# Three more token tiles of a gated block's input turned on VectorE and through DRAM, with the work around them put in another order

## The chip, the core and the metric

The kernel runs on one core of one Trainium2 chip. A core has five engines, each with a queue of its own that is worked off strictly in order: TensorE (PE, matmuls into PSUM; the profile shows its weight loads apart, as PEld), VectorE (DVE), ScalarE (ACT), GpSimd (POOL) and SyncE (SP, which here only issues DMA transfers). Engines wait for one another through semaphores. The metric is the time of one execution on the device in microseconds (us); lower is better. Every number below that has no other source is from the profile or the trace of the kernel before.

## The reference

One layer of a hybrid block over 1040 tokens (16 learned meta tokens ahead of 1024 real ones), width 1024, all in float32:

```python
mix = mixer(rms_norm(h, pre_mix_norm), w_in, ..., w_out)     # short convolutions, a gate, layer norm
h = h + rms_norm(mix, post_mix_norm)
ff = swiglu(rms_norm(h, pre_ffn_norm), w_gate, w_up, w_down) # silu(xn @ w_gate) * (xn @ w_up) @ w_down
h = h + rms_norm(ff, post_ffn_norm)
return h[:, N_META:, :]
```

`w_gate` and `w_up` are 1024 x 2816, `w_down` is 2816 x 1024. The change lies at the seam between the mixer's output projection (`w_out`) and the gate's two matrix products.

## The kernel before

**Arithmetic.** Every float32 operand is kept as two parts, a rounded `hi` and a rest `lo = x - hi`; a product is three matmuls (hi*hi, lo*hi, hi*lo; `mm3`, lines 107 to 109). The rounding is a cast on ScalarE, the rest a subtraction on VectorE, so each operand of TensorE costs one instruction on either engine. The products of the gate and of `w_down` are done by a scheme of the Strassen-Winograd kind: the operands are cut into 2 x 2 blocks, and seven products of sums of blocks replace eight.

**Up to the seam.** The 1024 tokens are eight tiles of 128. `group` (line 852) multiplies the mixer's output `y` (`yh`, `yl`) by `w_out` for a few token tiles at a time: tiles 0 to 2, then 3 to 5, then 6 and 7. The contraction runs over eight blocks k of 128; for each k there are 12 matmuls for two tiles. A dictionary gives a function to run ahead of step 0, 1, 2, ... of that loop; step 6 stands for the last two blocks, which are done tile by tile. `group` ends with `leave_psum`: ScalarE takes the sum of squares of each PSUM bank (line 621), VectorE multiplies it by a gain (line 622), and the bank is free. Tile 7's two sums lie in banks 7 and 4 (`OUT_BANKS`).

`norms` then makes two RMS norms of each tile and adds the residual: line 643 on VectorE, the squares of line 645 on ScalarE, and line 651 on VectorE, which gives the gate's input `hn` of the tile with tokens on the partitions.

**Turning.** The gate's products need `hn` with channels on the partitions. Tiles 0, 1 and 2 are turned by `send`, `fetch` and `receive`: VectorE transposes 32 x 32 blocks (line 669), SP writes the tile to DRAM (`xd`, line 670), four DMAs read it back with the blocks in their places into the same `hn` tile (line 675), and ScalarE copies it into `raw` (line 685) and, for the upper channel half of tiles 0 to 3, also makes `B11`'s hi and lo (lines 683, 684). Tiles 3 to 7 are turned by TensorE in `turn`: eight transposes each (line 659) into a PSUM bank, copied out by ScalarE (lines 661, 663). Tile 3's transposes stand ahead of step 5 of `group((6, 7))`, those of tiles 4 and 5 ahead of its step 6 (`early`), those of 6 and 7 behind the third product of the gate.

**The gate's products.** `raw[q, g]` are the blocks of the turned input (q: channel half, g: token half), called `r11`, `r21`, `r12`, `r22`. `Pair(j)` holds 128 columns of `w_gate` (m = 0) and of `w_up` (m = 1) from either half; 11 pairs. `order` is the order written out by hand of the 77 steps s = (pair, product): the seven products of pairs 0 and 1 alternate, then each pair has its seven in a row. A step is 24 matmuls, 12 for m = 0 and 12 for m = 1. Its weights side is made `LEAD = 2` steps ahead by `a_side(s)`: sums of blocks on VectorE, the cast on ScalarE (line 710), the rest on VectorE (line 697). Its right side is one of seven pairs of tiles `X[n]`: `X[1] = B11`, `X[2] = B21` (a hi and lo of `r21`), `X[6] = T2`, and so on. The results leave PSUM a step later (`results`, `Pair.leave`); the gate itself is `glu`: a Silu on ScalarE and a product, on GpSimd. In the text below, "step 0" is pair 0's product 1, step 1 pair 1's product 1, steps 2 and 3 product 2 of each (on `B21`), steps 4 and 5 product 6 (on `T2`, made of all eight tiles).

Step 1 writes banks 7 and 4, those that tile 7 of `group((6, 7))` leaves. Steps 2 and 3 add onto the banks of steps 0 and 1, so that ScalarE must first have copied these out (line 794).

**What sets the order.** Every engine's queue is written out by hand: instructions stand in each queue in the order in which the program makes them (`manual_schedule`). Buffers come from pools with a fixed number of places; an instruction that first writes a new tile waits until a place of that pool has been left by all users of the old tile, also by those that the program makes later on other queues. Four pools matter here:

- `tp`, tag "t", 5 places of one token tile each: `gB_post` and `gB_ffn` (the two gains, used by lines 622 and 651 to the end of `norms((6, 7))`), the `hn` tiles, and some of the weights of the pairs: by the condition in `Pair.load` the `w_up` block of pair 1's first half (`u11` below) is one.
- `wp`, tag "ws", 3 places: raw rows of `w_out`, and the other weights of pairs 0 and 1. Pair 0's two blocks and pair 1's `w_gate` block take the places that rows 5, 6 and 7 of `w_out` leave when they are split (`split_o`, lines 161 and 162).
- `yap`, the places of `y`; `xg` and `rp`, places of 8 KB a partition for `raw`, the `X` tiles and others.

## Time and profile before

| | |
|---|---|
| median of 3 runs | 963.99 us (963.87 to 964.51) |
| the profiled execution, its own time | 964.56 us |
| its span in the profile | 962.8 us |
| granted TensorE clock | 0.999 |
| DVE, ACT, POOL busy | 76%, 42%, 27% of the span |

The profile's page, its views by window and line, the waits and the chain of waits are all of that one execution. Times in the views are us from the start of the span. A row of the timeline is: start, length, engine and line, operation, out<-in by the program's names, shapes, how many instructions are merged (the length is then that of all of them), and in brackets the idle time of the engine before it and what ended that. The page gives a matmul of 512 columns 0.39 us; consecutive ones start 0.227 us apart, since they are pipelined.

### The profile page before, as it was taken

The page shows a single profiled execution, that of the slowest core. Times are in us where ns is not written, and L with a number is a line of the kernel's source. Part 1 is how long each engine was busy: PE and PEld are TensorE (multiplying, and loading weights), DVE is VectorE, ACT ScalarE, POOL GpSimd, SP SyncE. Part 2 cuts the span into 40 slices and gives each one's busy share as a digit, 9 for nine tenths or more (in the row PEclk, how much of TensorE's full clock was granted, in tenths as well). Part 3 has the DMA queues.
Part 4 walks back from the last instruction along what each step waited for, and adds up shares of the span by engine and source line. Part 5 has one row for each costly group of instructions (what it writes and reads, how often), then busy time and mean ns, then how long its engine had stood idle before and what let it go on. Part 6 is the DMA issues. An engine that isn't in the chain of part 4 may idle for free.

```text
span 962.8 us, 12522 instructions
## 1 busy us (share of the span) xinstructions
PE 954.6 (99%) x4570; PEld 820.2 (85%) x4570; DVE 735.4 (76%) x1022; ACT 405.2 (42%) x666; POOL 260.1 (27%) x225
## 2 busy tenths in 40 slices
PE   9999999999999999999999999999999999999997
PEld 9999999998888888888888888888888888888885
DVE  6699999886476799999987787887886543546775
ACT  8533423365446653453443343333433333322341
POOL 1277954552000000204134133132242111111210
PEclk9999999999999999999999999999999999999999
DMA  8011111114447510555532633624419899856866
GB/s 312 23 45 46 65 45 44 66 44 151 134 155 250 185 67 1 186 228 173 222 151 106 225 125 117 238 91 152 154 39 366 295 356 365 260 175 212 319 205 247
DMA packets 60878, 159.83 MB, mean 166 GB/s; under 512 B 6417, under 2 KB 8977, under 8 KB 60817
## 3 DMA queue, kind: packets, MB, share of 16 engines
q1 hardware_dynamic: 44352, 106.98, 30.8%
q0 software_dynamic: 11088, 40.38, 13.1%
q10 hardware_dynamic: 5376, 11.67, 3.4%
q8 instruction: 36, 0.59, 0.3%
q14 instruction: 26, 0.20, 0.1%
HBM read 108.67 MB, written 50.33 MB: 165 GB/s over the span
## 4 chain that ended last, share of the span: by engine, by line
PE 98%; DMA 1%; DVE 0%; SPq 0%; ACT 0%; issue 0%; DVEq 0%
PE x L108 8%; PE x L109 8%; PE x L107 8%; PE y L108 6%; PE y L109 6%; PE y L107 6%; PE qx L108 4%; PE qx L107 4%; PE qx L109 4%; PE qy L108 3%; PE qy L107 3%; PE qy L109 3%; PE po L107 3%; PE po L109 3%; PE po L108 3%; PE p_c L107 2%
## 5 line engine op out<-in xcount | busy, mean ns | idle before, releaser
L697 DVE TENSOR_TENSOR op<-u,op 128x512 fp32r<-128x512 f32 x154 | 141.6, 951 | 27.8 <-ACT op L710 26.7
L710 ACT CAST op<-u 128x512 fp32r<-128x512 f32 x154 | 92.0, 619 | 133.2 <-DVE u L697 75.2
L697 DVE TENSOR_TENSOR db<-wb,db 128x512 fp32r<-128x512 f32 x77 | 54.0, 704 | 86.2 <-ACT db L1174 85.9
L700 POOL TENSOR_TENSOR C<-C,C 128x512 f32<-128x512 f32 x11 | 17.3, 1569 | 322.9 <-ACT C L822 210.7
L1174 ACT CAST db<-wb 128x512 fp32r<-128x512 f32 x77 | 47.3, 621 | 119.7 <-PE qx L109 57.2
L107 PE MATMUL qx<-db,a 128*128 128x512 f32 x176 | 68.5, 389 | 0.0
L108 PE MATMUL qx<-db,a 128*128 128x512 f32 x176 | 68.5, 389 | 0.0
L109 PE MATMUL qx<-db,a 128*128 128x512 f32 x176 | 68.5, 389 | 0.0
L694 DVE TENSOR_TENSOR U<-y,U 128x512 f32<-128x512 f32 x66 | 43.5, 682 | 17.0 <-PE y L109 17.0
L700 POOL TENSOR_TENSOR U<-U,U 128x512 f32<-128x512 f32 x21 | 30.1, 1434 | 86.9 <-ACT U L822 60.5
L108 PE MATMUL qy<-db,a 128*128 128x512 f32 x132 | 51.5, 390 | 0.0
L109 PE MATMUL qy<-db,a 128*128 128x512 f32 x132 | 51.4, 389 | 0.0
L107 PE MATMUL qy<-db,a 128*128 128x512 f32 x132 | 51.3, 389 | 0.0
L1054 POOL DMA_DIRECT2D a<-gdS x44 | 23.2, 528 | 91.4 <-PE qx L109 45.6
L382 DVE SCALAR_TENSOR_TENSOR ac<-g,pr,ac 128x512 f32<-128x512 f32 x56 | 42.0, 750 | 0.0
L382 DVE SCALAR_TENSOR_TENSOR ae<-d,pr,ae 128x512 f32<-128x512 f32 x56 | 42.0, 750 | 0.0
L107 PEld LDWEIGHTS qx<-db,a 128*128 128x128 f32 x176 | 33.0, 188 | 6.9
L109 PEld LDWEIGHTS qx<-db,a 128*128 128x128 f32 x176 | 33.0, 188 | 6.9
L108 PEld LDWEIGHTS qx<-db,a 128*128 128x128 f32 x176 | 33.0, 188 | 6.8
L697 DVE TENSOR_TENSOR u<-u,u 128x512 f32<-128x512 f32 x44 | 38.0, 884 | 0.8
L1054 POOL DMA_DIRECT2D a<-gdA x33 | 17.8, 539 | 61.7 <-PE qx L109 26.8
L107 PE MATMUL x<-B21h,op 128*128 128x512 f32 x88 | 34.3, 390 | 0.0
(358 smaller groups left out, 2928.0 us busy)
## 6 DMA issues: line engine op xcount, KB each, us to landing
a<-gdS POOLq DMA_DIRECT2D x44, 512.0 KB, 4.5
a<-gdA POOLq DMA_DIRECT2D x33, 512.0 KB, 5.8
u<-w_gate_u SPq DMA_DIRECT2D x22, 512.0 KB, 5.4
u<-w_up_u SPq DMA_DIRECT2D x22, 512.0 KB, 6.2
gdS<-HI SPq DMA_DIRECT2D x44, 256.0 KB, 2.4
gdA<-HI SPq DMA_DIRECT2D x33, 256.0 KB, 2.0
gdS<-GS SPq DMA_DIRECT2D x33, 256.0 KB, 2.7
ws_o<-w_out_u SPq DMA_DIRECT2D x14, 512.0 KB, 4.6
```

The costliest lines, as they stand in the source:

```text
L107: nc.tensor.matmul(o, lh, rh, start=start, stop=False, skip_group_check=again)
L108: nc.tensor.matmul(o, lh, rl, start=False, stop=False, skip_group_check=again)
L109: nc.tensor.matmul(o, ll, rh, start=False, stop=stop, skip_group_check=again)
L382: nc.vector.scalar_tensor_tensor(out if i == n - 1 else acc, src[:, i : i + HALF], w(i), init if i == first else acc, op0=ALU.mult, op1=AL ...
L694: (eng or nc.vector).tensor_tensor(o, a, b, op=ALU.add)
L697: (eng or nc.vector).tensor_tensor(o, a, b, op=ALU.subtract)
L700: (eng or nc.vector).tensor_tensor(o, a, b, op=ALU.mult)
L710: nc.scalar.copy(t[:, 0, :], src)
L1054: nc.gpsimd.dma_start(loads[n, j], gd[an][j])
L1174: nc.scalar.copy(t[:, 0, :], b)
```

## The change

- **Turning.** Tiles 3, 4 and 5 go the way of tiles 0 to 2. `norms` hands its last products (line 651) back as a list for this group, so that tile 3's product and transpose come first and tiles 4 and 5 follow inside `group((6, 7))`: step 1 has the split of row 5 of `w_out` and tile 5's product, step 2 the split of row 6, the loads of pair 0, the four reads of tile 3 and tile 4's transpose and write, step 3 the split of row 7, a load of pair 1 and tile 5's transpose and write. The reads of tiles 4 and 5 are issued in `early`, behind the load of `u11`; `receive(3)` is in `early`, `receive(4)` and `receive(5)` where the cast of `B21` was. The transposed tiles `xt` take places that `y` leaves.
- **B21** is cast and its rest made at the end of `early`, ahead of `leave_psum` in the queues, in place of inside `norms((6, 7))`. The sums `t1_sum` of the first two column blocks move from `early` to behind `a_side(3)`.
- **Pairs 0 and 1** multiply their gate on VectorE in place of GpSimd.
- **Operand sums ahead of results:** from step 3 on, `a_side(s + 2)` is cut in two; its sums and casts (`a_high`) stand ahead of the results of step s - 1, its rests (`a_low`) stay behind them.
- **Places:** `y` lies in a pool `rp` of four places that stays open (tag of `big`), `rq` has one, and `T2`, `B22` and a block of `w_down` are given to other pools.

```diff
         side_of(a).tensor_tensor(cv[a], cv[a], rS, op=ALU.mult)
 
     def after_b(a):
-        yh[a], yl[a] = (yap.tile([P, SEQ], F32R, tag="y", name=f"y{c}{a}") for c in "hl")
+        y = big(f"y{a}", pool=rp)
+        yh[a], yl[a] = y[:, :SEQ], y[:, SEQ:]
         for q in range(2):
             s = slice(q * HALF, (q + 1) * HALF)
             nc.vector.tensor_tensor(cv[a][:, s], pu["b", a][:, q, :], cv[a][:, s], op=ALU.mult)
...
         if i == 0:
             fs.close()
             ya = ExitStack()
-            yap = ya.enter_context(tc.tile_pool(name="yap", bufs=8, side="right"))
+            rp = ctx.enter_context(tc.tile_pool(name="rp", bufs=4, side="right", reuse_waits="tile"))
     assert next(conv_taps, 0) == 0
     split_o(1, nc.gpsimd)
     load_o(2)
...
         nc.sync.dma_start(h, x[i * P : (i + 1) * P, :])
         return h
 
-    def norms(grp, left, s1, hs, between=None, first=None):
-
+    def norms(grp, left, s1, hs, between=None, first=None, parts=False):
         n_ = len(grp)
         v = sm.tile([P, 16], F32, tag="s2", name=f"pm{grp[0]}")
         nc.vector.tensor_tensor(v[:, :n_], s1[:, 0:n_], s1[:, 4 : 4 + n_], op=ALU.add)
...
         if between:
             between()
         r = rsqrt_n(v2[:, :n_], 1.0 / D, RMS_EPS, n_, f"pf{grp[0]}")
-        for q, i in enumerate(grp):
-            nc.vector.scalar_tensor_tensor(n[i], hs[i], r[:, q : q + 1], gB["ffn"], op0=ALU.mult, op1=ALU.mult)
+        last = [lambda q=q, i=i: nc.vector.scalar_tensor_tensor(n[i], hs[i], r[:, q : q + 1], gB["ffn"], op0=ALU.mult, op1=ALU.mult) for q, i in enumerate(grp)]
+        if parts:
+            return n, last
+        for f in last:
+            f()
         return n
 
     def turn(i, n, at=(0, 1)):
...
                 nc.tensor.transpose(pt[:, k * P : (k + 1) * P], n[:, (4 * q + k) * P : (4 * q + k + 1) * P], ident)
             p4 = pt.rearrange("p (a b) -> p a b", a=4)
             nc.scalar.copy(raw[q, i // 4][:, :, c], p4)
-            if (q, i // 4) == (0, 0):
-                nc.scalar.copy(B11[0][:, :, c], p4)
-                nc.vector.tensor_tensor(B11[1][:, :, c], p4, B11[0][:, :, c].bitcast(F32), op=ALU.subtract)
-
-    xd = {i: dram.tile([P, D], F32, tag=f"xd{i}", name=f"xd{i}") for i in range(3)}
+
+    xd = {i: dram.tile([P, D], F32, tag=f"xd{i}", name=f"xd{i}") for i in range(6)}
 
     def send(i, n, t):
         nc.vector.transpose(t.rearrange("p (j k q) -> p j k q", j=4, k=8), n.rearrange("p (k j q) -> p j k q", k=8, j=4))
...
             nc.sync.dma_start(n[32 * j : 32 * j + 32].rearrange("r (i x) -> r i x", i=4), src)
 
     def receive(i, n):
-        c = slice(i * P, (i + 1) * P)
+        c = slice((i % 4) * P, (i % 4 + 1) * P)
         split4 = lambda t: t[:, :, c].rearrange("p k (i q) -> p k i q", i=4)
         for q in range(2):
             n4 = n.rearrange("p (i k q) -> p k i q", i=4, k=8)[:, 4 * q : 4 * q + 4]
-            if q == 0:
+            if q == 0 and i < 4:
                 nc.scalar.copy(split4(B11[0]), n4)
                 nc.vector.tensor_tensor(split4(B11[1]), n4, split4(B11[0]).bitcast(F32), op=ALU.subtract)
-            nc.scalar.copy(split4(raw[q, 0]), n4)
+            nc.scalar.copy(split4(raw[q, i // 4]), n4)
 
     st = None
     free = [5, 6, 7, 4, 0, 1, 2, 3]
...
             if m == 0:
                 nc.scalar.activation(v[c, 0], v[c, 0], AF.Silu)
             else:
-                mul(v[c, 0], v[c, 0], v[c, 1], None if (self.j, c) == (NP - 1, "U2") else nc.gpsimd)
+                mul(v[c, 0], v[c, 0], v[c, 1], None if self.j < 2 or (self.j, c) == (NP - 1, "U2") else nc.gpsimd)
 
         def split(self, *names):
 
...
 
     hs = {i: residual_x(i) for i in (3, 4, 5)}
     s1, left = group((3, 4, 5), middle, {1: ahead(0, 5), 2: ahead(1, 6), 3: lambda: [ahead(2, 7)(), back(0)()], 4: back(1), 5: back(2)})
-    hn = norms((3, 4, 5), left, s1, hs)
+    hn, last_mul = norms((3, 4, 5), left, s1, hs, parts=True)
+
+    def turned(i):
+        t = big(f"xt{i}", F32, rp)[:, :D]
+        send(i, hn[i], t)
+
+    last_mul[0]()
+    turned(3)
+    last_mul[1]()
 
     n_hi = [0]
     X = {1: B11}
...
 
     order = [(j, n) for n in (1, 2, 6, 5, 7, 3, 4) for j in range(2)]
     order += [(j, n) for j in range(2, NP) for n in (1, 6, 2, 5, 7, 3, 4)]
-    made, sums = {}, {}
+    made, high, sums = {}, {}, {}
     LEAD = 2
 
-    def a_side(s, *places):
+    def a_high(s, *places):
         if s >= len(order) or s in made:
             return
         j, n = order[s]
         if j > 1 and n == 1 and j + 1 < NP:
             pairs[j + 1] = Pair(j + 1)
         src = sums.pop(s, None) or [pairs[j].a_side(n, m) for m in range(2)]
-        t = [operand_hi(src[m], f"{n}_{j}{m}", places[m] if places else None) for m in range(2)]
-        for m in range(2):
-            sub(t[m][:, 1, :], src[m], t[m][:, 0, :].bitcast(F32))
-        made[s] = t
-
-    def pairs_load():
+        made[s] = [operand_hi(src[m], f"{n}_{j}{m}", places[m] if places else None) for m in range(2)]
+        high[s] = src
+
+    def a_low(s):
+        for m, src in enumerate(high.pop(s, ())):
+            sub(made[s][m][:, 1, :], src, made[s][m][:, 0, :].bitcast(F32))
+
+    def a_side(s, *places):
+        a_high(s, *places)
+        a_low(s)
+
+    def step1():
+        ahead(5)()
+        last_mul[2]()
+
+    def step2():
+        split_o(6)
+        pairs[0].load(0)
+        fetch(3, hn[3])
+        turned(4)
+
+    def step3():
         split_o(7)
         pairs[1].load(0, (0,))
+        turned(5)
 
     def early():
         for q in range(2):
             raw[q, 1] = blocks(big(f"raw{q}1", F32))
-        turns(4, 5, at=(5, 6))()
         pairs[1].load(0, (1,))
-        for i in range(2):
-            t1_sum(i)
+        for i in (4, 5):
+            fetch(i, hn[i])
+        back(3)()
         a_side(0)
         a_side(1, (hp, "h"), (jp, "jk"))
+        X[2] = pair("B21", (rp, rp))
+        copy_hi(X[2], raw[1, 0])
+        split_lo(X[2], raw[1, 0])
 
     hs = {i: residual_x(i) for i in (6, 7)}
-    s1, left = group((6, 7), up, {1: ahead(5), 2: lambda: [split_o(6), pairs[0].load(0)], 3: pairs_load, 5: turns(3), 6: early})
+    s1, left = group((6, 7), up, {1: step1, 2: step2, 3: step3, 6: early})
     r11, r21, r12, r22 = raw[0, 0], raw[1, 0], raw[0, 1], raw[1, 1]
-    X[2] = pair("B21", (None, None))
     T2r = blocks(big("T2r", F32))
     results = {s: pairs[order[s][0]].product(order[s][1], made.pop(s)) for s in range(2)}
 
     def between():
         pairs[0].load(1)
         results[0]()
-        split_lo(X[2], r21)
         a_side(2)
 
-    hn = norms((6, 7), left, s1, hs, between, lambda: copy_hi(X[2], r21))
+    turned_back = hn
+    hn = norms((6, 7), left, s1, hs, between, lambda: [receive(i, turned_back.pop(i)) for i in (4, 5)])
     del left, hs
     table(AF.Silu)
     ya.close()
     p2.close()
-    rp = ctx.enter_context(tc.tile_pool(name="rp", bufs=5, side="right", reuse_waits="tile"))
+    rq = ctx.enter_context(tc.tile_pool(name="rq", bufs=1, side="right", reuse_waits="tile"))
     st = ctx.enter_context(tc.tile_pool(name="st", bufs=11, reuse_waits="tile"))
-    X[6] = pair("T2", (rp, rp))
+    X[6] = pair("T2", (rq, None))
     a_side(3)
-    for f in (t2_sum, t2_hi, t2_lo):
+    for f in (t1_sum, t2_sum, t2_hi, t2_lo):
         for i in range(2):
             f(i)
 
...
 
     def b22():
         T4.append(blocks(big("T4h")))
-        X[3] = pair("B22", (rp, None))
+        X[3] = pair("B22", (None, None))
         copy_hi(X[3], r22)
         split_lo(X[3], r22)
 
...
     def load_b(b, g):
 
         n_ = min(4, NP - 4 * g)
-        pool = {(0, 0): bp, (0, 1): bp, (0, 2): rp, (1, 0): rp, (2, 1): rp, (2, 2): rp, (3, 1): rp}.get((b, g))
+        pool = {(0, 0): bp, (0, 1): bp, (0, 2): rq, (1, 0): rp, (2, 1): rp, (2, 2): rp, (3, 1): rp}.get((b, g))
         t = WB[b, g] = blocks(big(f"wb{b}{g}", F32, pool))
         src = w_down[4 * g : 4 * g + n_, :, b // 2, b % 2 * 512 : (b % 2 + 1) * 512]
         for k in range(n_) if b == 0 else (slice(0, n_),):
...
         if s == len(order) - 1:
             load(1, "A11", 2, "ws")
             load(1, "A11", 3, "wh")
+        if s > 2:
+            a_high(s + LEAD)
         results.pop(s - 1, lambda: None)()
         if s == 2:
             for f in (t1_sum, t2_sum):
...
                 load(1, "A11", q, "ws")
         for f in extra.get(s, ()):
             f()
-        a_side(s + LEAD)
+        a_low(s + LEAD)
         if s in (13, 16):
             pairs[s == 16].sums()
         if s in first_splits:
```

## The prediction, made before the changed kernel was run

> **What bounds the kernel now.** First the page: its share of busy time, then the chain of work that ended last.
>
> ```profile
> span 962.8 us, 12522 instructions
> PE 954.6 (99%) x4570; PEld 820.2 (85%) x4570; DVE 735.4 (76%) x1022; ACT 405.2 (42%) x666; POOL 260.1 (27%) x225
> ...
> PE 98%; DMA 1%; DVE 0%; SPq 0%; ACT 0%; issue 0%; DVEq 0%
> ```
>
> Next PE's waits, all of them:
>
> ```profile
> PE warm L89 <- DVE pr L113: 1.1, 1, 1.1
> PE p_g L108 <- DVE xl L179: 0.3, 1, 0.3
> ```
>
> Both are on its first matmuls (`warm`, and `p_g`, the first unit). After that TensorE waits for nobody, so the kernel is as long as TensorE's list of work: an instruction taken off PE shortens it by its step, as long as nothing makes PE wait, and any new wait of PE is added in full. A view by windows then says how near such waits are.
>
> ```profile
> 340.00:360.00 20.00, 20.00 (x98) 16.77 (x97) 19.50 (x31) 12.69 (x22) 0.00 (x0) 1.00 0.22 79
> ```
>
> Its columns are the window's sum, then busy us (instructions) of PE, PEld, DVE, ACT and POOL, the granted clock and the DMA's share: VectorE is busy for 19.5 of 20 us. At the seam the kernel is balanced between PE and the VectorE-ScalarE chain.
>
> **What is taken from PE.** The chain lists the transposes by tile:
>
> ```profile
> 314.61 0.87 PE pt L659 x8
> ...
> 318.24 1.75 PE pt L659 x16
> ...
> 341.78 1.75 PE pt L659 x16
> ```
>
> The first two rows go: 0.87 + 1.75 = 2.62 us. [...]
>
> PE's own times, first matmul of `group((6, 7))`, of steps 0, 1 and 4, and the second of step 5:
>
> ```profile
> 300.85 0.39 PE L107 MATMUL po<-wh_o,yh 128*128 128x512 f32 x1
> ...
> 325.30 0.39 PE L107 MATMUL x<-B11h,op 128*128 128x512 f32 x1
> ...
> 330.74 0.39 PE L107 MATMUL x<-B11h,op 128*128 128x512 f32 x1
> ...
> 348.84 0.62 PE L777 MATMUL y<-T2h,op 128*128 128x512 f32 x2
> ...
> 354.50 0.39 PE L108 MATMUL y<-T2l,op 128*128 128x512 f32 x1
> ```
>
> A step of 24 matmuls takes 330.74 - 325.30 = 5.44 us. Without the transposes PE would be ready for step 0 at 325.30 - 2.62 = 322.7. I now walk the queues to see when its inputs are.
>
> **Tile 3 arrives late.** VectorE before:
>
> ```profile
> 280.31 3.49 DVE L669 STREAM_TRANSPOSE jk<-hn 128x1024 f32<-128x1024 f32 x3
> ...
> 309.36 3.68 DVE L651 SCALAR_TENSOR_TENSOR hn<-h,r_pf,gB_ffn 128x1024 f32<-128x1024 f32 x3
> 312.95 3.49 DVE L162 TENSOR_TENSOR wl_o<-ws_o,wh_o 128x1024 fp32r<-128x1024 f32 x3
> ...
> 325.93 2.48 DVE L622 TENSOR_TENSOR jk<-po,gB_post 128x512 f32<-128x512 f32 x4
> ...
> 331.83 2.35 DVE L697 TENSOR_TENSOR B21l<-raw,B21h 128x1024 fp32r<-128x1024 f32 x2
> ```
>
> From the starts of successive rows a product costs 1.20, a transpose 1.14, a split of `w_out` 1.14. From 309.36 the queue is now product 3, transpose 3 (0.1 wait for it), product 4, split 5, product 5, split 6: split 6 ends at 316.6 instead of 315.3. Split 7 follows transpose 4, ends at 318.85, and holds PE's row 7 by 0.1. SP before:
>
> ```profile
> 316.85 0.42 SPq L739 DMA_DIRECT2D u<-w_up_u  x1
> ...
> 338.98 0.33 SPq L739 DMA_DIRECT2D u<-w_up_u  x1
> ```
>
> and how long these two kinds take from issue to landing, the reads in the whole trace, the loads from 310 to 345:
>
> ```profile
> L675 SPq DMA_DIRECT2D hn<-xd x12: 376/432/1356, 284.3 to 290.9; - x12
> ...
> DMA to landing us min/median/max: 3.8/4.5/5.0
> ```
>
> ```profile
> L739 SPq DMA_DIRECT2D u<-w_up_u x4: 328/330/425, 315.3 to 343.6; - x4
> ...
> DMA to landing us min/median/max: 3.3/4.1/7.8
> ```
>
> The four reads of tile 3 stand on SP behind pair 0's second load, which takes the place that split 6 leaves: issued 316.6, the reads at 0.43 us each until 318.3, the last landed 4.5 us later, 322.8. ScalarE before:
>
> ```profile
> 291.31 1.14 ACT L685 COPY raw<-hn 128x512 f32<-128x512 f32 x2
> ...
> 324.67 0.62 ACT L710 CAST op<-u 128x512 fp32r<-128x512 f32 x1 [1.71 <-DMA u<-w_up_u]
> 325.20 0.59 ACT L621 ACTIVATE sq<-po 128x512 f32<-128x512 f32 x1
> ...
> 325.78 0.59 ACT L621 ACTIVATE sq<-po 128x512 f32<-128x512 f32 x1
> ...
> 328.72 1.98 ACT L937 CAST B21h<-raw 128x1024 fp32r<-128x1024 f32 x2
> 330.75 1.06 ACT L645 ACTIVATE hn<-h 128x1024 f32<-128x1024 f32 x1
> ...
> 333.00 1.05 ACT L794 COPY U<-x 128x512 f32<-128x512 f32 x2
> 333.95 1.15 ACT L710 CAST op<-u 128x512 fp32r<-128x512 f32 x2
> ```
>
> `receive(3)` is a cast and two copies, 322.9 to 324.5. Only behind them stands step 0's first cast, 324.5 to 325.1. PE starts step 0 at 325.1 and waits 0.5 more for the rest (one VectorE subtraction): 2.4 + 0.5 us. The gain is gone here.
>
> **The buffer of `u11`.** Before, it was issued at 316.85, with no wait, because tile 3 had left its `hn` place at PE's transposes. Now `gB_post`, `gB_ffn` and `hn` 3, 4, 5 fill the five places of `tp` until `receive(3)` has read its tile, so the load goes out at 324.5. That such a load waits for a place is seen before: the one of 338.98 started when the last user of `gB_ffn` ended:
>
> ```profile
> 337.67 1.28 DVE L651 SCALAR_TENSOR_TENSOR hn<-h,r_pf,gB_ffn 128x1024 f32<-128x1024 f32 x1
> ```
>
> (338.95). With the median of 4.1 us `u11` lands at 328.6 instead of 324.65. Its cast is in ScalarE's queue, and behind it stand, now, `B21`'s two casts (1.98) and the squares of `leave_psum` (0.58 apart): cast 328.7, `B21h` 329.2 to 331.2, squares from 331.1, tile 7's first 332.25 to 332.95. VectorE has the same order: rest of `u11`, `B21l` until 332.6, then line 622; tile 7's first bank is free at 334.45. Before, this was at 327.8. Step 1 writes that bank, and PE was ready at 331.1: a wait of 3.4 us.
>
> **The norms of tiles 6 and 7.** From tile 7's last bank (335.05; before 328.41) the chain is: sum and root 1.0; then ScalarE's four copies of tiles 4 and 5 (4 x 0.57 = 2.3, in place of `B21`'s 1.98), the two squares, 2.25 as from 330.75 to 333.00, two copies of step 0's banks 0.95, the casts of step 2: first at 341.5. `B21l` is no longer in that chain, but VectorE waited there for the squares anyway. Step 1 ends 334.5 + 5.44 = 339.9, so PE waits 1.6, and 0.5 for the rest. Step 2 and tiles 6 and 7's transposes run to 349.2. Step 3 needs the copy of step 1's banks, which stands behind `T2`'s first casts on ScalarE, and these wait for VectorE: products of tiles 6 and 7 until 346.0, step 3's rests 1.2, `t1_sum` 1.2 (moved here), `T2r`: copy done 350.8, wait 1.6. Step 4 needs `T2h` of the last columns; from `T2r`'s first subtraction to it VectorE's work is as before:
>
> ```profile
> 340.07 1.29 DVE L697 TENSOR_TENSOR T2r<-raw,raw 128x512 f32<-128x512 f32 x2
> ...
> 347.24 1.22 ACT L920 CAST T2h<-T2r 128x512 fp32r<-128x512 f32 x2 [1.19 <-DVE T2r L697]
> ```
>
> 8.4 us, with small waits 8.55: 348.35 + 8.55 = 356.9, PE ready 0.7 earlier. Step 5: with its four sums ahead of step 2's results, VectorE's product of line 802 waits for the Silu, which now stands behind two casts; its rest is late by 1.2 us.
>
> **Sum.** Waits 0.1 + 2.4 + 0.5 + 3.4 + 1.6 + 0.5 + 1.6 + 0.7 + 1.2 = 12.0; less the transposes, 2.6, and about 0.2 of small waits before that fall away: **+9.2 us**. The check by time: the second matmul of step 5 moves from 354.50 to about 363.8.
>
> **The other two edits** come too late to give it back, since PE has no slack to catch up with afterwards. Before, GpSimd's six products held VectorE up, and VectorE waited for casts:
>
> ```profile
> 381.43 1.61 POOL L700 TENSOR_TENSOR C<-C,C 128x512 f32<-128x512 f32 x1 [148.80 <-ACT C L822]
> ```
>
> ```profile
> 381.20 2.38 DVE L697 TENSOR_TENSOR u<-u 128x512 f32<-128x512 f32 x2
> ...
> 395.09 1.98 DVE L697 TENSOR_TENSOR op<-u,op 128x512 fp32r<-128x512 f32 x2 [0.61 <-ACT op L710]
> ```
>
> 2.38 against 1.28 for two: 1.1 us lost beside one GpSimd product, against one more product of 0.6 on VectorE and its wait for the Silu. Gain at most 0.5 each, and up to 0.6 a step by the earlier casts. Those gains keep steps 6 to 19 free of waits (each rest ready 1 us or more ahead), no more; without them the 0.1 to 0.2 of step 12 would return. Of the unknown: `u11`'s landing 3.3 to 7.8 (-0.8 to +3.7), tile 3's reads 3.8 to 5.0 (-0.7 to +0.5). I take the medians.
>
> **Rivals.**
> 1. *`u11` finds a place at once* (against it: the five users; for it: before, it never waited). Issued at 320.4, on the chip by 325: step 1's wait shrinks to 0.8, the sum to +6.6: 970.6.
> 2. *`u11` is slowed by the eight reads of tiles 4 and 5*, issued right behind it: 7.8 as at 316.85, +12.9: 976.9.
> 3. *The clock falls in the long wait of step 1.* If PE ran at half rate afterwards for as long as it stood, 3.4 us, that costs 1.7 more: 974.9. Against it: the granted clock is 1.00 in all rows, which hold no such wait. [...]
> 4. *The turning hides, as it did for tiles 0 to 2*, and PE keeps 2.6 + 0.2: 961.2. This takes step 0's cast by 322.7, so tile 3's reads landing within 2.2 us of issue (the least is 3.8), and line 622 done with tile 7 by 328.1 instead of 334.4. If my order of the queues is wrong so far, half of it would be no change, 964.
>
> **The numbers.** Forecast 0.58 (971.9 to 975.0), rival 1 0.14, rival 2 0.08, rival 3 0.07, faster 0.08, no change 0.05. The profiled execution took 964.56, 0.57 above the median of the runs shown; 964.56 + 9.2 = 973.8, against the median 973.2, which I give. Range 967 to 977.5: rivals 1 to 3 and, below 970, a walk wrong by half. A measurement of this kernel can tell 0.2%, 1.9 us, from no change: faster 0.08, same 0.05, slower 0.87.
>
> **What would show it.** PE waits in the changed profile, none before: at step 0 for a cast, at step 1 for line 622, at steps 2 and 3 for ScalarE. A row "op<-u [.. <-DMA u<-w_up_u]" on ScalarE that ends near 328.6; the issue of that load behind `receive(3)`. No `pt` rows but the 16 of tiles 6 and 7; VectorE idle between 320 and 323. It is wrong if step 0 starts by 323, if `u11` is issued near 320, or if line 622's last product of tile 7 ends before 330.

## The result and the profile after

| | before | changed |
|---|---|---|
| median of 4 runs each | 964.19 us (963.87 to 964.51) | 975.79 us (974.66 to 976.70) |
| ratio, 95% interval | | 1.0118 [1.0103, 1.0134] |
| span of the profiled execution | 962.8 us | 974.6 us |
| second and third matmul of step 5 | 354.50, 354.73 | 365.39, 366.48 |

The changed kernel is 1.2% slower; the prediction was 973.2 us, range 967 to 977.5. First the page of the changed kernel, then all waits of PE (total us, times, longest):

```profile
span 974.6 us, 12468 instructions
PE 957.1 (98%) x4546; PEld 820.8 (84%) x4546; DVE 729.5 (75%) x1031; ACT 406.0 (42%) x666; POOL 254.7 (26%) x219
...
PE 93%; DVE 3%; ACT 1%; DMA 1%; issue 1%; SPq 0%; DVEq 0%; ACTq 0%
```

```profile
PE x L107 <- ACT op L710: 4.8, 1, 4.8
PE x L107 <- DVE jk L623: 2.5, 1, 2.5
PE x L107 <- ACT U L794: 1.4, 1, 1.4
PE warm L89 <- DVE pr L113: 1.1, 1, 1.1
PE y L109 <- DVE op L697: 0.7, 1, 0.7
PE y L777 <- ACT T2h L928: 0.2, 1, 0.2
```

PE has its 24 instructions less (4570 - 4546), and is busy 2.5 us longer all the same. In order of time the new waits are: step 0 for its first cast (4.8), step 1 for line 623, which is line 622 of before and empties tile 7's bank (2.5), step 3 for ScalarE's copy of step 1's banks (1.4), step 4 (0.2) and step 5 (0.7). The chain of work that ended last (start, length, what) left PE at 300.37, where the norms of tiles 3 to 5 begin, and came back to it 59 us later, at step 4:

```profile
300.13 0.24 PE po L109
...
318.47 7.07 DMA hn<-xd
325.75 0.41 issue
326.16 1.14 ACT raw L685 x2
327.32 4.49 DMA u<-w_up_u
331.88 0.49 issue
332.36 1.05 ACT B21h L945
333.44 2.36 DVE B21l L697 x2
335.80 2.39 DVE jk L623 x4
...
339.01 1.66 ACT raw L685 x3
...
347.51 1.28 DVE hn L650
...
359.54 5.57 PE y L777 x24
```

The last of tile 3's reads lands at 318.47 + 7.07 = 325.5, `receive(3)` empties the tile, `u11` is issued at 327.32 and lands at 331.8, 7.2 us later than before (324.65); behind it come the casts of `B21`, line 623, the norms of tiles 6 and 7 and the two parts of `T2`, without a wait for any other transfer, until step 4 starts at 359.54, 10.7 us later than before (348.84).

The view by windows (PE, PEld, DVE, ACT, POOL, granted clock, the DMA's share, GB/s) shows two more things, here before:

```profile
320.00:324.00 4.00, 4.00 (x19) 3.27 (x19) 2.70 (x5) 2.42 (x5) 0.00 (x0) 1.00 0.58 221
324.00:328.00 4.00, 4.00 (x19) 3.32 (x18) 2.68 (x5) 2.94 (x9) 0.00 (x0) 1.00 0.00 1
```

and in the changed kernel:

```profile
316.00:320.00 4.00, 3.98 (x18) 2.95 (x18) 4.00 (x4) 0.00 (x0) 0.00 (x0) 1.00 0.98 357
320.00:324.00 4.00, 3.11 (x14) 2.25 (x12) 0.07 (x1) 0.00 (x0) 0.00 (x0) 1.00 1.03 255
324.00:328.00 4.00, 0.13 (x1) 0.13 (x1) 0.84 (x2) 2.36 (x5) 0.00 (x0) 0.98 0.75 298
328.00:332.00 4.00, 4.00 (x11) 3.16 (x12) 1.74 (x3) 1.08 (x3) 0.00 (x0) 0.59 0.91 254
...
336.00:340.00 4.00, 2.35 (x6) 1.86 (x7) 3.70 (x10) 2.37 (x8) 0.00 (x0) 0.76 0.00 0
340.00:344.00 4.00, 4.00 (x16) 3.19 (x15) 1.69 (x2) 3.93 (x9) 0.00 (x0) 0.81 0.69 262
```

The DMA engines, done at 324 before, are now busy for 0.75 to 1.03 of the time from 316 to 332 (the share as the view prints it). And the granted clock falls twice, in the first part of step 0 and of step 1. From the starts of successive matmuls between 295 and 372 us: gaps of more than 0.7 us add 9.9 us, matmuls 0.427 apart instead of 0.227 add 2.8, smaller ones 1.6 more than before, and the transposes take 2.6 away: 11.7, of the 11.75 by which step 5's third matmul moved.

### The profile page after: what moved, and what is told of

Read it like the earlier page. It is cut to its first block, busy times and chain, and to the rows that moved or that the text cites. A ratio compares the mean times of both kernels' runs of the same rounds, so it can differ in the third digit from the quotient of the medians.

```text
span 974.6 us, 12468 instructions
## 1 busy us (share of the span) xinstructions
PE 957.1 (98%) x4546; PEld 820.8 (84%) x4546; DVE 729.5 (75%) x1031; ACT 406.0 (42%) x666; POOL 254.7 (26%) x219
## 4 chain that ended last, share of the span: by engine, by line
PE 93%; DVE 3%; ACT 1%; DMA 1%; issue 1%; SPq 0%; DVEq 0%; ACTq 0%
PE x L107 7%; PE x L109 7%; PE x L108 7%; PE y L109 6%; PE y L107 6%; PE y L108 6%; PE qx L109 4%; PE qx L108 4%; PE qx L107 4%; PE qy L108 3%; PE qy L109 3%; PE qy L107 3%; PE po L107 2%; PE po L108 2%; PE po L109 2%; PE p_v L108 2%
## 5 line engine op out<-in xcount | busy, mean ns | idle before, releaser
L710 ACT CAST op<-u 128x512 fp32r<-128x512 f32 x154 | 94.0, 621 | 206.5 <-DVE u L697 101.4
L697 DVE TENSOR_TENSOR op<-u,op 128x512 fp32r<-128x512 f32 x154 | 123.0, 837 | 28.2 <-ACT op L710 28.2
L700 POOL TENSOR_TENSOR U<-U,U 128x512 f32<-128x512 f32 x17 | 28.3, 1666 | 59.6 <-ACT U L822 43.8
L107 PE MATMUL x<-B11h,op 128*128 128x512 f32 x88 | 35.8, 407 | 7.2 <-ACT op L710 4.8
L108 PE MATMUL x<-B11l,op 128*128 128x512 f32 x88 | 35.5, 403 | 0.0
```

The costliest lines, as they stand in the source:

```text
L107: nc.tensor.matmul(o, lh, rh, start=start, stop=False, skip_group_check=again)
L108: nc.tensor.matmul(o, lh, rl, start=False, stop=False, skip_group_check=again)
L697: (eng or nc.vector).tensor_tensor(o, a, b, op=ALU.subtract)
L700: (eng or nc.vector).tensor_tensor(o, a, b, op=ALU.mult)
L710: nc.scalar.copy(t[:, 0, :], src)
```

## The experiments

Where nothing else is said, each is an edit on the changed kernel. "Time" is the median, with the ratio to the kernel before as run beside it on the same chip.

**The two other edits alone** (on the kernel before).

```diff
-                mul(v[c, 0], v[c, 0], v[c, 1], None if (self.j, c) == (NP - 1, "U2") else nc.gpsimd)
+                mul(v[c, 0], v[c, 0], v[c, 1], None if self.j < 2 or (self.j, c) == (NP - 1, "U2") else nc.gpsimd)
...
+        if s > 2:
+            a_high(s + LEAD)
         results.pop(s - 1, lambda: None)()
...
-        a_side(s + LEAD)
+        a_low(s + LEAD)
```

> The kernel before with only two of the four edits: pairs 0 and 1 multiply their gate on VectorE, and from step 3 on the operand sums and casts stand ahead of the results. Turning and B21 as before. Theory (the time is TensorE's list plus its waits, and the waits of the changed kernel come from tile 3's late reads and the queue behind them): these edits give TensorE nothing to do earlier, since it had no waits; the sums ahead of step 2's results put two casts ahead of the Silu on ScalarE, so that step 5's rest is late by about 1.2 us. Before + 0.6 to + 1.4 us, one wait of TensorE near 354 for a subtraction of VectorE, no other. Rival (the operand sums and the missing GpSimd products are what costs in the changed kernel): + 4 us or more. A third reading, that they are a gain in themselves: - 0.5 us or less.

964.46 us, ratio 1.0003 [0.9994, 1.0012]: no change, and PE waits nowhere in the seam. The wait in step 5 that was expected with them did not come: it needs a step 4 that is late already (the last experiment takes this up). So the loss comes with the turning and what was moved with it.

**Tile 3's reads first.**

```diff
-        pairs[0].load(0)
         fetch(3, hn[3])
+        pairs[0].load(0)
         turned(4)
```

> The changed kernel with one thing moved: the four reads of tile 3 are issued ahead of pair 0's two loads in place of behind them. Theory (tile 3's reads come late, and all that follows hangs on them): the reads are issued near 315 in place of 317.06, land near 321.5 in place of 325.5, step 0 waits until 325 (now for pair 0's second weights as much as for tile 3) in place of 327.9, u11 is issued near 323.5, and the time falls by 2 to 3 us, to about 973. Rival (the falls of the clock to half cost the time): still two waits of TensorE over 2 us, so the clock falls as often and the time stays within 0.7 us of the changed kernel's.

976.06 us, ratio 1.0123 [1.0109, 1.0136]: no gain, where 2 to 3 us were expected; the rival, the clock, had no change as well, and is tested by itself below. The reads landed at 321.5 and step 0 started at 323.88, 4 us sooner. It was worth nothing:

```profile
323.33 7.83 DMA u<-w_up_u
...
358.89 5.58 PE y L777 x24
```

`u11` was issued 4 us sooner too, took 7.83 us instead of 4.49, and landed 0.65 us sooner, at 331.16. Step 4 moved by the same 0.65. The step 0 wait of 4.8 us was only exchanged for one of 7.1 in step 1.

**A place for `u11`.** Tile 3's reads land in the tile that `left[3]` leaves, so that tile 3's place in `tp` is free once its transpose has been made.

```diff
+    landing = left[3]
...
-        fetch(3, hn[3])
+        fetch(3, landing)
...
-        back(3)()
+        hn.pop(3)
+        receive(3, landing)
```

> The changed kernel with another landing place for tile 3: the reads go into the tile of tile 3's first norm, which is free, so that its hn place is free after the transpose and the load of u11 does not wait for receive(3). Theory: u11 is issued near 320.9 in place of 327.3 and lands near 329.5 in place of 331.8 (the DMA engines are full then); its cast ends the stall of ScalarE's queue 2 us sooner, line 623 leaves bank 7 2 us sooner, step 1 starts near 335.3 in place of 337.65, and the time falls by 1.5 to 2.5 us, to about 973.8. If the place of u11 is not what holds step 1, the time stays as it is within 0.5 us. Rival (clock): no change as long as two long waits remain.

975.08 us, ratio 1.0114 [1.0099, 1.0130]: mostly a miss.

```profile
322.31 8.00 DMA u<-w_up_u
...
358.11 5.58 PE y L777 x24
```

With the place free, the load goes out 5.0 us sooner and lands 1.5 us sooner. The prediction's cause, the wait for a place, is there in the trace, but taking it away gives back 0.7 us by the medians, less than the 2 us over which the changed kernel's runs lie. The 1.5 us too is hardly more than the spread between single profiles: three kernels below that issue their transfers in the changed kernel's order (matmuls in the waits, B21's split back, the sums behind the results) landed this load at 331.26, 331.69 and 330.56, the changed one at 331.81. What holds `u11` is then, as far as this run goes, that it stands last in line at DMA engines that are full (share 1.03 at 320 to 324 above). Two of the runs that follow change the traffic around it.

**Matmuls in the waits.** Products whose result nobody reads, 22 ahead of step 0 and 10 ahead of step 1, keep PE busy.

```diff
+    for s, b in ((0, 0), (1, 1)):
+        idle = bank(b, f"idle{s}")
+        for q in range((22, 10)[s]):
+            nc.tensor.matmul(idle, yh[7][:, :P], yl[7][:, :512], start=q == 0, stop=q == (22, 10)[s] - 1)
```

> The changed kernel with extra matmuls that nobody reads, on two unused PSUM banks: 22 ahead of step 0 and 10 ahead of step 1 (about 5.0 and 2.3 us at 0.227 each), so that TensorE works through its two long waits. It computes the same. Theory (steps 1 and 2 wait for VectorE and ScalarE anyway, and the half clock only uses up time that would have been waited): no fall of the granted clock in 327 to 342, and the time within 0.6 us of the changed kernel's 975.8. Rival (the two falls, 3.4 us at half clock each, cost 1.7 us apiece): the time falls by 2.5 to 3.4 us, to about 972.8.

975.85 us, ratio 1.0122 [1.0108, 1.0136]. The clock now stays whole,

```profile
328.00:332.00 4.00, 4.00 (x18) 3.12 (x17) 1.46 (x4) 1.23 (x3) 0.00 (x0) 1.00 0.99 265
332.00:336.00 4.00, 3.79 (x17) 2.82 (x15) 3.74 (x5) 4.00 (x10) 0.00 (x0) 1.00 0.63 123
```

and the time is the same. Step 0 and step 1 are faster, and step 2 then starts 1.2 us late for want of its operand, where it did not wait at all in the changed kernel: 2.8 us of half clock were paid inside a chain that PE is not on. The clock as a cause is refuted.

**`u11` ahead of two writes.** On the kernel with the place: tiles 4 and 5 are turned as before, but written to DRAM behind `u11`'s load, a megabyte less ahead of it.

```diff
-        turned(4)
+        turned(4, False)
...
         pairs[1].load(0, (1,))
+        for i in (4, 5):
+            nc.sync.dma_start(xd[i], xt[i])
```

> Edit on e3_u11_place: the turned tiles 4 and 5 are still turned by VectorE at the same places, but their two writes to DRAM (0.5 MB each) are issued behind the load of the second half of w_up's blocks of pair 1, no longer ahead of it. The reads of tile 3 and everything that is computed stay. Theory A (the DMA engines are full, and this load lands when all bytes issued ahead of it have been moved, some 260 GB/s): one megabyte less ahead of it, so it lands near 326.5 instead of 330.3, step 1 begins near 333 instead of 336.2, and the time is some 2.5 to 4 us below e3's, 971 to 972.5 us, ratio 1.0075 to 1.0095; tiles 4 and 5 come back later, at some 340, still ahead of the norms' end. Theory B (the load is late for its own issue, or step 1 hangs on ScalarE's order of work): the load lands within 1 us of 330.3 and the time stays at 974.5 to 975.5 us.

973.03 us, ratio 1.0089 [1.0076, 1.0103], between the two. The load went out at 319.4 and landed at 328.3, 2.0 us sooner than with the place alone and 1.8 later than theory A had it. Step 1 waited for nothing. But the chain had changed hands:

```profile
319.86 9.71 DMA xd<-xt
...
332.80 3.57 DMA hn<-xd
...
356.50 5.58 PE y L777 x24
```

The first of the postponed writes took 9.7 us, the last of tile 5's reads landed at 336.4, not at 340, and ScalarE's copies of them hold up the norms. My expectation that tiles 4 and 5 would still be early was wrong. So in these two kernels the traffic around the load decides when it lands, not its place in `tp`, and pushing a part of that traffic back makes others late. Whether the bytes ahead of the load count, or those right behind it, this run does not separate: here the eight reads of tiles 4 and 5, too, went out only after the load had landed (from 329.59 on; with the place alone, from 324.89). Of the 2.0 us, 1.6 lie in the last stretch: the load landed 1.26 us after the transfer issued ahead of it, with the place alone 2.87 us after.

**Tile 3 back on TensorE**, tiles 4 and 5 as changed.

```diff
-    turned(3)
...
-        fetch(3, hn[3])
...
-        back(3)()
...
-    s1, left = group((6, 7), up, {1: step1, 2: step2, 3: step3, 6: early})
+    s1, left = group((6, 7), up, {1: step1, 2: step2, 3: step3, 5: turns(3), 6: early})
```

> Tile 3 alone goes back to TensorE (8 transposes, 0.9 us of TensorE, ScalarE's copies out of PSUM), tiles 4 and 5 stay on VectorE and DRAM, the rest as in the changed kernel. Theory A (bytes ahead of the load): a megabyte less, and step 0 waits for nothing that lands; the load of pair 1 lands at about 326, step 1 begins at some 331 instead of 337.65, so that the time is 5 to 6.5 us below the changed kernel plus 0.9 for the transposes: 970 to 971.5 us. Theory of the prediction (the load waits for the place that tile 3's arrival empties): here the place is free at once, and the same gain follows or a little more, 969 to 970 us. Rival (the two waits are one in another dress: what tile 3 no longer takes, tiles 4 and 5 take): 974 to 976 us.

971.84 us, ratio 1.0078 [1.0064, 1.0092]: 4.0 us back, although PE has 0.9 us of transposes again. Step 0 starts at 323.52 without a wait.

```profile
319.26 7.92 DMA u<-w_up_u
...
354.92 5.78 PE y L780 x24
```

The gain is less than theory A and the prediction's theory had (970 to 971.5 and 969 to 970 us), and more than the rival's, because the load, though issued 8 us sooner, still takes 7.92 us. From its landing at 327.18 to step 4 it is 27.7 us, as in every kernel so far whose chain runs over it:

| kernel | `u11` issued | landed | step 4 starts | between |
|---|---|---|---|---|
| changed | 327.32 | 331.81 | 359.54 | 27.7 |
| tile 3's reads first | 323.33 | 331.16 | 358.89 | 27.7 |
| a place for `u11` | 322.31 | 330.31 | 358.11 | 27.8 |
| tile 3 on TensorE | 319.26 | 327.18 | 354.92 | 27.7 |

Issue times 8 us apart end 4.6 us apart, and step 4 follows the landing by the same 27.7 us, whatever PE waits for in between.

**B21's split back inside the norms.**

```diff
-        X[2] = pair("B21", (rp, rp))
-        copy_hi(X[2], raw[1, 0])
-        split_lo(X[2], raw[1, 0])
...
+    X[2] = pair("B21", (rp, rp))
...
         results[0]()
+        split_lo(X[2], r21)
```

> Only the split of B21 goes back inside the norms of the last two tiles, as in the kernel before; the rest as changed. Theory A (step 1 is late by the load, and ScalarE's 2.0 us of casts behind it add to it): step 1 begins some 2 to 2.5 us sooner, at about 335.3, but the casts then stand in the chain of the norms and step 2 waits about 2 us more: the time is 974.8 to 975.8 us, no change against the changed kernel. Rival (the early split is what costs): 971 to 972.5 us. Rival (the early split pays for itself): 977 to 978 us.

974.54 us, ratio 1.0106 [1.0091, 1.0122], not to be told from the changed kernel's 1.0118. Step 1 starts at 334.90, 2.75 us sooner, and step 2 now waits 2.9: the casts are in the chain in either place, ahead of line 623 or inside the norms. Step 4 comes 1.0 us sooner in the profile.

**B21's split first.** On the kernel with tile 3 on TensorE (lines are 3 higher there): the split ahead of the operands of steps 0 and 1, so that its casts run while ScalarE waits for the loads.

```diff
+        X[2] = pair("B21", (rp, rp))
+        copy_hi(X[2], raw[1, 0])
+        split_lo(X[2], raw[1, 0])
         a_side(0)
         a_side(1, (hp, "h"), (jp, "jk"))
-        X[2] = pair("B21", (rp, rp))
-        copy_hi(X[2], raw[1, 0])
-        split_lo(X[2], raw[1, 0])
```

> Edit on e6_tile3_pe (tile 3 on TensorE, tiles 4 and 5 through DRAM): the split of B21 is written ahead of the operands of steps 0 and 1 instead of behind them, nothing else. Theory A (after the bytes, the order on ScalarE decides: B21's two casts of 2.0 us stand between the cast of the last load and the squares that empty step 1's bank): the casts now go into time in which ScalarE waits for loads, step 1 begins near 331.0 instead of 333.0, and the time is 1.5 to 2 us below e6's: 969.8 to 970.4 us. Rival (step 1 hangs on the landing of the load alone): no change, 971.4 to 972.2 us.

969.00 us, ratio 1.0050 [1.0036, 1.0064]: 2.8 us less, more than the 1.5 to 2 expected.

```profile
319.22 7.69 DMA u<-w_up_u
326.93 0.63 ACT op L713
327.59 0.69 DVE op L700
328.28 2.40 DVE jk L623 x4
...
352.03 5.81 PE y L780 x24
```

The load lands as before it (326.91), and line 623 follows its operand with no `B21` row between: 25.1 us to step 4 instead of 27.7. The early split, as the change has it, does cost; what it costs depends on whether it stands ahead of the late load's cast or behind it.

**Two tiles, behind the loads.** Tile 3 on TensorE; the loads of pairs 0 and 1 and of the residual's last two tiles first, then tiles 4 and 5 turned, written and read; `B21` split first; the sums back behind the results; `t1_sum` ahead of step 2's operand.

```diff
     def step3():
         split_o(7)
-        pairs[1].load(0, (0,))
-        turned(5)
+        pairs[1].load(0)
+        for i in (6, 7):
+            hs[i] = residual_x(i)
+        for i in (4, 5):
+            last_mul[i - 3]()
+            turned(i)
+        for i in (4, 5):
+            fetch(i, hn[i])
```

> Another order: tile 3 on TensorE, all loads of w_up for pairs 0 and 1 and of x's last two tiles issued first, then tiles 4 and 5 are turned by VectorE, written and read, and come back inside the norms of the last two tiles; B21 split early, VectorE has the products of pairs 0 and 1. Theory A: no load that a step needs has other bytes ahead of it, so that none of the first steps waits, and 16 transposes of 0.109 us leave TensorE: 962.0 to 963.0 us against 964.2, ratio 0.9975 to 0.999. Rival (any turning through DRAM here costs more than the transposes, by ScalarE's copies in the chain of the norms): step 2 waits 0.5 to 2 us and the time is 964 to 966 us.

966.90 us, ratio 1.0028 [1.0018, 1.0038]: slower than before, as the rival had it, and by more than its 964 to 966. Steps 0 and 1 wait for nothing; step 2 waits 2.4 us. ScalarE shows why (last bracket: idle before, and what ended it):

```profile
329.24 1.14 ACT L688 COPY raw<-hn 128x512 f32<-128x512 f32 x2 [2.86 <-DMA hn<-xd]
331.63 1.14 ACT L688 COPY raw<-hn 128x512 f32<-128x512 f32 x2 [1.25 <-DMA hn<-xd]
332.68 1.06 ACT L645 ACTIVATE hn<-h 128x1024 f32<-128x1024 f32 x1
```

It stood for the reads of tile 4 (2.86 us) and then of tile 5 (1.25), with the squares of the norms (line 645) queued behind. In the kernel before they ran at 330.75.

**The copies later.** On that kernel: the reads land where the turned tiles stood (`xt`), and the four copies and `t1_sum` stand behind step 3's operand.

```diff
-            fetch(i, hn[i])
+            fetch(i, xt[i])
...
-    hn = norms((6, 7), left, s1, hs, between, lambda: [receive(i, turned_back.pop(i)) for i in (4, 5)])
+    hn = norms((6, 7), left, s1, hs, between)
...
     a_side(3)
-    for f in (t2_sum, t2_hi, t2_lo):
+    for i in (4, 5):
+        receive(i, xt.pop(i))
+    for f in (t1_sum, t2_sum, t2_hi, t2_lo):
```

> Edit on e7_two_tiles: the reads of tiles 4 and 5 land where the turned tiles stood, no longer in the places of the normalized tiles, and ScalarE's four copies of them, with the differences T1 = B12 - B11 that need them, stand behind the operand of step 3, no longer ahead of the squares of the norms. Theory (in e7 ScalarE stood at 331 us waiting for the reads, with the norms' squares and the operand of step 2 queued behind it): step 2 no longer waits its 2.4 us and TensorE's clock does not fall; what remains is 16 transposes less, 1.7 us: 962.0 to 963.0 us, ratio 0.998 to 0.999. Rival (the copies and differences now stand ahead of step 4's operand, which becomes late): step 4 waits 0.5 to 1.5 us, 963.0 to 964.5 us.

963.30 us (962.86 to 963.62) beside 964.37, ratio 0.9989 [0.9980, 0.9998]: 0.1% faster than the kernel before, and 12.5 us faster than the changed one. The expected ratio was 0.998 to 0.999. Of 1.7 us of transposes it keeps 1.1; part of the rest went into two small waits that the kernel before does not have, the last two of these lines:

```profile
PE warm L89 <- DVE pr L113: 1.1, 1, 1.1
PE p_g L108 <- DVE xl L179: 0.4, 1, 0.4
PE y L780 <- ACT T2h L931: 0.2, 1, 0.2
PE x L107 <- ACT U L797: 0.2, 1, 0.2
```

**The sums behind the results again.**

```diff
-        if s > 2:
-            a_high(s + LEAD)
         results.pop(s - 1, lambda: None)()
...
-        a_low(s + LEAD)
+        a_side(s + LEAD)
```

> The changed kernel with one edit undone: the sums and casts of the operand two steps ahead stand behind the results of the step before again, together with the rests. Theory (as the prediction had it for step 5: with the sums ahead, VectorE's product with the Silu and the rest of step 5's operand come late, so that TensorE waits some 0.9 us in step 5 more): that wait goes, all up to step 4 stays (step 4 at about 359.5 in the span), and the time is 0.7 to 1.2 us below the changed kernel: 974.6 to 975.1 us, span 973.4 to 973.9. Rival (the order costs nothing, as it cost nothing in the kernel before, where no step waits; the wait in step 5 comes of the late T2 alone): 975.5 to 976.1 us, the same wait in step 5.

975.05 us (974.03 to 975.71) beside 963.91, ratio 1.0118 [1.0101, 1.0135]: by the ratio no difference from the changed kernel. By the trace there is one: PE waits in step 4 last (0.2 us) and no longer in step 5. Step 4 in the chain:

```profile
358.30 5.75 PE y L777 x24
```

From there to the end of the span it is 972.3 - 358.3 = 614.0 us, as before (962.8 - 348.84), against 615.1 in the changed kernel and 615.0 to 615.1 in the seven other profiles above that kept its order. I take the 1.1 us as real in the profile. That it is in the time was not shown: the runs of either kernel lie up to 2 us apart.

## Why the prediction was right, and where it was not

The time (975.8 against 973.2) lies in the range, but above the forecast's own 971.9 to 975.0. None of the three signs of being wrong came: step 0 started at 327.87, `u11` was issued at 327.32, and line 623 (622 of before) was done with tile 7 at 338.19. Step by step:

- **What bounds the kernel**, PE's list of work with no slack behind it: right. Span and third matmul of step 5 moved by the same 11.8 us.
- **Transposes, 2.6 us**: 24 PE instructions went. The kernel with two tiles through DRAM and hardly a wait shows that most of such a gain can be kept: 1.1 of 1.7 us. Of the 0.2 us of small waits that were to fall away with them, the trace of before has 0.1.
- **"The last landed 4.5 us later, 322.8"**: a mis-sized term. Issued as walked (318.47 against 318.3), the reads took 6.9 to 7.1 us, not the 3.8 to 5.0 of tiles 0 to 2:

```profile
L675 SPq DMA_DIRECT2D hn<-xd x4: 424/428/432, 317.1 to 318.5; - x4
...
DMA to landing us min/median/max: 6.9/7.1/7.1
```

  The range of before came from a stretch in which only the three tiles' own writes stood ahead of the reads; here two tiles of the residual and two loads, half a megabyte each, were under way when the reads were issued, and landed between 317.2 and 323.5. The row that the prediction quoted for the loads, 3.3 to 7.8, already had the longer times of this very stretch in it (its four loads issued from 314 to 317 took 4.3 to 7.8), and I took the medians. Step 0 waited 4.8 us instead of 2.4, and its cast started at 327.2 instead of 324.5.
- **"The buffer of `u11`", issued 324.5, landing 328.6**: the order was right (behind `receive(3)`, issue 327.32), the landing was 331.8, 3.2 us late (2.0 to 3.2 in the four profiles with this order of transfers). As a cause it was wrong: with a place at once (my rival 1, 970.6) the load left at 322.3, landed at 330.3, and the time was 975.1. Issued early or late, the load then waited for the DMA engines; without tile 3's write and reads, a megabyte less, the load landed at 327.2. And with tile 3's reads back by 321.5, sooner than walked, it still landed at 331.2: what was too small is the time that the transfers of this stretch need together, not that of the reads alone.
- **From `u11`'s landing to step 4**: walked as 356.9 - 328.6 = 28.3 us, measured 27.7, and 27.7 to 27.8 in the six kernels that keep this order behind it. The queues behind the load (cast, `B21h`, squares, line 622, the norms, `T2`) were right to 0.6 us. So the error of the sum, 11.8 - 9.2 = 2.6, is the late landing, 3.2, less this 0.6. The terms ahead of step 4 came out otherwise one by one, as the next lines show; that they add up is because the chain behind the landing, not each wait of PE, sets step 4.
- **Step 1, 3.4 us**: 2.5, since step 0 itself ended late, its first eight matmuls at half clock. **Step 2, 1.6 + 0.5**: none in the changed kernel, since step 1 in turn ran at half clock until 341.5; with the clock kept up the wait came back, 1.2. **Steps 3 and 4, 1.6 and 0.7**: 1.4, and 0.2 with a slow start.
- **Step 5, 1.2 us**: 0.7 us and the start of the matmul, 0.86 above the usual distance, at the third matmul and not the second: the rest of an operand is first used by line 109. The edit that I blamed, sums ahead of results, is what brings the wait in the traces, but only in kernels whose step 4 is late. The check by time named the second matmul, which this wait does not move.
- **The other two edits give nothing back**: right, 1.0003 alone.
- **Rival 2** (7.8 us for `u11`, by the reads behind it): in the changed kernel it took 4.49, with two transfers still under way ahead of it. The time of this rival, 976.9, is nearer to the measured one than my forecast, but not by its way. Whether the reads behind the load cost it something stays open (see the kernel with `u11` ahead). **Rival 3, the clock**: it fell to half after both long waits (4.8 and 2.5 us), for 3.4 us each, and cost nothing: 975.85 us in the kernel where it did not fall. **Rival 4** (the turning hides): only with two tiles and another order of transfers and copies.

## What to carry over

Take a transfer's time from rows in which the same bytes are in flight: the row with the spread (3.3 to 7.8) is a warning that the median belongs to another stretch. When a new transfer joins a stretch where the DMA engines are near full, look for the load that is last in line and follow the queues from its landing; waits ahead of it, places and the clock may all change with no effect on the time. Work that waits for a transfer belongs behind everything on its engine that does not wait for one: moving four copies on ScalarE behind the next operands, and their reads to another place, was worth 3.6 us in the kernel with two tiles.

## What the runs showed of the hardware

- **Half clock after waits of 4.8, 2.5 and 2.4 us.** In the changed kernel's trace the granted clock is 0.5 from 327.84 to 331.25 and from 338.08 to 341.49, 3.41 us each, and matmuls go 0.427 us apart there, not 0.227. The first stretch began with the restart from a wait of 4.8 us (5.14 between matmul starts), the second 0.4 us after the restart from one of 2.5 us (2.85 between starts). In the kernel with two tiles behind the loads a wait of 2.4 us was followed by the same, with matmuls 0.43 us apart until 340.46:

```profile
320.00:330.00 10.00, 10.00 (x46) 8.29 (x45) 9.29 (x18) 4.00 (x12) 0.00 (x0) 1.00 0.87 291
330.00:340.00 10.00, 7.55 (x27) 5.54 (x26) 4.81 (x10) 8.32 (x16) 0.00 (x0) 0.85 0.48 169
```

  After shorter waits it was not seen: in the kernel with `B21`'s split first, with waits of 1.0, 1.1 and 1.4 us, the granted clock is 1.00 in every window from 310 to 370. No run has a wait between 1.4 and 2.4 us at the seam. How long the clock stays low is not set by the wait alone: after 4.8 us it was 3.41 us in the changed kernel; in the kernel with `u11` ahead, whose wait was 4.8 us too, the granted clock is 0.83 over 320 to 330 and 0.82 over 330 to 340, an estimated 7 us at half (0.17 + 0.18 of 10 us, divided by the missing half).
- **At most eight of SP's transfers under way**, in the traces of the kernel before and of the changed kernel: none of SP's 308 and 323 transfers was issued with more than seven others of its queue still to land, and 23 and 27 of them with just seven. The eight reads of tiles 4 and 5 stand behind `u11`, 0.43 us each, and yet their row is 1 us longer than eight of these:

```profile
327.32 0.33 SPq L739 DMA_DIRECT2D u<-w_up_u  x1
327.71 4.43 SPq L675 DMA_DIRECT2D hn<-xd  x8
```

  The seventh went out at 330.55, the eighth at 331.83, when `u11`, the eighth ahead of it, had landed (331.81). In the kernel with a place for `u11` that load, expected at 320.9, went out at 322.31, just after the landing (322.29) of the one issued at 316.22, which is the eighth ahead of it, too. No run was made for this alone; that the number under way is what held these transfers was not shown.
